# A gated delta rule's chunk inverse with half-column levels, applied once to the values less the state's part

## The chip, the cores and the metric

The kernel runs as one program on one core of a Trainium2 chip. The metric is device time in microseconds (us), the median of several executions.

## The reference

One step of a one-layer hybrid encoder: a combined input projection, latent attention (8 heads), a gated delta rule (4 heads, keys and values of width 128), an output projection and an MLP. It covers a prompt of 16 + 2048 rows and 64 rows of a running stream. The change lies in the delta rule, which the reference evaluates in chunks of `C` rows (the kernel uses 18 chunks: 16 of 128 rows, one of 16, one of 64):

```python
gc = jnp.cumsum(blocks(g), axis=-1)
decay = jnp.exp(jnp.where(causal, gc[..., :, None] - gc[..., None, :], -jnp.inf))
kb = kc * bc[..., None]
a = jnp.where(strict, jnp.einsum('...id,...jd->...ij', kb, kc) * decay, 0.0)
t_inv = lax.linalg.triangular_solve(eye + a, ..., lower=True)      # inverse of I + a
u = t_inv @ (vc * bc[..., None])
w = t_inv @ (kb * jnp.exp(gc)[..., None])
qk = jnp.einsum('...id,...jd->...ij', qc, kc) * decay
def step(S, xs):
    v_new = u_i - w_i @ S
    o = (q_i * jnp.exp(g_i)[..., None]) @ S + qk_i @ v_new
    S = S * jnp.exp(g_last)[..., None] + einsum('bhck,bhcv->bhkv', k_i * jnp.exp(g_last - g_i)[..., None], v_new)
```

## The kernel before

The program runs in stages: input projection (to about 540 us), the delta rule (540 to 966 us), attention over the prompt, attention of the stream, and output projection with MLP. The delta rule is written as generators that a loop in `phase_g` advances by one step a round. `gdn_prep` is independent of the state, and up to four chunks of it are in flight; a new one starts every six rounds. `gdn_scan` carries the state from chunk to chunk, one scan at a time in six steps. The loop also advances the attention's query projection (`q_gen`, 17 tiles, to about 760 us) and then its first keys. The order of a round is only the order in which code is written; a scheduler in the compiler then orders each engine's instructions by its own estimate, and the engines run their queues in that order.

The names: `lev` are the inverse's levels, `tt` and `uu` (`t`, `u` in the code) the inverse so far and its transpose in f16, each for the 4 heads side by side (128 x 512). `m_lv` are 0/1 masks of the levels' blocks. `gpp` (5 buffers) and `gps` (2) are PSUM tiles of the preparation and of the scan. `bn` is minus the masked product of keys with its decay, `bh` and `bl` its f16 high and low part. `dm` are the decays, `lg` the factor from which a product makes their exponents. `kn` are the normalised keys, `kneg` the same times minus the decay, `wt` the inverse applied to `kneg`, `vn` the values, `uf` the finished inverse in f32, `kd` the keys that update the state `S`, `vw` the new values, `o` and `fr` the output and its norm.

A chunk's preparation has six levels (L526 to L541): a product `bh` by `t` (L530), a predicated copy into the next level (L531), two products (L535, L537), and two copies out of PSUM, `t` on ScalarE (L539) and `u` on VectorE (L540). Then a correction makes `uf` (L557), and a product with `kneg` makes `wt` (L561, L563). The scan adds two products in PSUM, `uf` by `vn` (L581) and `wt` by the state (L582), and scales the sum into `vw` (L584).

Of the kernel before, what the change touches and what calls it, by code (L numbers as in the profile page):

```python
# [39 lines left out]
CHUNKS = list(range(NS)) + [17] + list(range(NS, 17))  # L40
# [4 lines left out]
NL = 2  # L45
GL, QLS = 17, 20
GB = {"kq": 4, "qk": 5, "kd": 5, "vn": 5, "uf": 5, "wt": 5, "ss": 5, "kv": 2, "sq": 1, "kn": 1, "lg": 1, "dm": 2, "db": 1, "bn": 1,
      "kneg": 3, "bh": 4, "bl": 4, "tt": 5, "uu": 5, "q16": 2, "rk": 3, "se": 1, "vw": 2, "S": 3, "o1": 1, "o": 1, "fr": 2}
GR, GK, GA, GF = 6, 4, 5, 2
QSB, QS = 2, 5  # L50
# [60 lines left out]
def bc1(ap, p, a, b):  # L111
    return ap.unsqueeze(1).to_broadcast([p, a, b])


def bc2(ap, p, a, b):
    return ap.unsqueeze(2).to_broadcast([p, a, b])


class Prog:
# [318 lines left out]
    def gdn_prep(self, n, P):  # L438

        nc, S = self.nc, self.S  # L440
        t0, C = chunk_span(n)
        sc = self.sc[n]
        want_o = n > 0
        cv = S["convT"].rearrange("(j p) t -> p j t", p=128)
        kv = self.gt("kv", 1, (128, 8, 128))
        nc.sync.dma_start(kv[:, :, :C], cv[:, 4:12, t0:t0 + C])
        kq = self.gt("kq", 2, (128, 4, 2, 128))
        nc.sync.dma_start(kq[:, :, 1, :C], cv[:, 0:4, t0:t0 + C])
        lg = self.gt("lg", 2)
        nc.gpsimd.tensor_tensor(lg[:C, :, :C], bc1(self.m_gt[:C, :C], C, 4, C), bc2(sc["g"][:C], C, 4, C), op=ALU.mult)  # L450
        yield
# [41 lines left out]
        for a in range(2):  # L493
# [31 lines left out]
        while s < C:
            y = lev[i]  # L526
            yield
            ps = self.gpsum()
# [12 lines left out]
            i, s = i + 1, 2 * s  # L541
# [22 lines left out]
        P.update(kq=kq, ss=ss, qk=qk, kd=kd, vn=vn, uf=uf, wt=wt)  # L564

    def gdn_scan(self, n, P):
# [46 lines left out]
        ss = P["ss"]  # L613
# [17 lines left out]
    def phase_g(self, g=True, q=True, eb=None):  # L631

        with ExitStack() as es:
# [1277 lines left out]
```

## Time and profile before

| what | value |
|---|---|
| median of 3 runs | 3350.31 us (3349.01 to 3351.44) |
| the profiled execution's own time, and its span | 3346.45 us, 3344.6 us |
| mean granted TensorE clock | 0.981 of full speed |
| busy, share of the span: PE, DVE, ACT, POOL | 96%, 81%, 47%, 12% |
| the chain that ended last, by engine | PE 84%, DVE 8%, ACT 2%, issue 2%, DMA 2%, POOL 1% |

The span goes from the first to the last instruction; the execution's own time holds 1.85 us more. PE is TensorE (PEld its weight loads), DVE VectorE, ACT ScalarE, POOL GpSimd. A matmul's duration in the trace holds its way through the array, and matmuls overlap; from the start of one to the start of the next is what it costs in a stream. An f32 matmul stands as two instructions.

### The profile page before, as it was taken

How to read it: one execution, taken by the hardware profiler on the slowest of the kernel's cores; microseconds unless marked ns; L12 is line 12 of the kernel's file. 1: busy time of each engine (PE TensorE's matmuls, PEld its weight loads, DVE VectorE, ACT ScalarE, POOL GpSimd, SP SyncE). 2: the span in 40 equal slices, each digit the busy share in tenths (PEclk: the TensorE clock that was granted, in tenths of full speed). 3: DMA queues.
4: the chain of work that ended last, by engine and by line, in shares of the span. 5: the costliest groups of instructions: out<-in, count | busy, mean ns of one | idle time of the engine just before them, and what ended most of it. 6: DMA issues, size and time to landing. Idle time of an engine off the chain costs nothing.

```text
span 3344.6 us, 54489 instructions
## 1 busy us (share of the span) xinstructions
PE 3218.6 (96%) x20037; PEld 2963.2 (89%) x20037; DVE 2693.3 (81%) x5438; ACT 1577.2 (47%) x3495; POOL 400.9 (12%) x758
## 2 busy tenths in 40 slices
PE   9999998998879999999999999999999999999999
PEld 6888887888867878887799999999999999999999
DVE  8877654888868778888689888888988888988887
ACT  5555534565536868787654233334332324422232
POOL 0110014565410000000201000001100002100000
PEclk9999998999989989999999999999999999999999
DMA  4322213233211011110332222234222224122222
GB/s 131 90 73 69 73 66 103 87 96 106 52 56 35 15 34 28 32 40 23 97 98 83 76 74 75 73 88 135 84 72 67 75 76 156 58 76 76 75 74 70
DMA packets 318091, 248.09 MB, mean 74 GB/s; under 512 B 31776, under 2 KB 291616, under 8 KB 317760
## 3 DMA queue, kind: packets, MB, share of 16 engines
q1 hardware_dynamic: 300256, 219.21, 22.5%
q10 hardware_dynamic: 15536, 16.23, 1.6%
q0 software_dynamic: 2032, 9.18, 0.8%
q8 instruction: 157, 2.57, 0.3%
q14 instruction: 110, 0.90, 0.1%
HBM read 196.99 MB, written 47.52 MB: 73 GB/s over the span
## 4 chain that ended last, share of the span: by engine, by line
PE 84%; DVE 8%; ACT 2%; issue 2%; DMA 2%; POOL 1%; ACTq 0%; SPq 0%; POOLq 0%; DVEq 0%
PE psu L1581 23%; PE psd L1581 21%; PE ps L270 5%; PE ps L271 5%; PE ps L272 5%; PE pss L974 2%; PE pso L991 2%; PE pss L975 2%; PE pso L993 2%; PE pss L976 2%; PE pso L992 2%; PE pspre L944 2%; DVE lev L531 1%; DMA qh<-mrow 1%; PE gpp L498 1%
## 5 line engine op out<-in xcount | busy, mean ns | idle before, releaser
L1581 PE MATMUL psu<-hh,uh 128*128 128x352 f32 x1728 | 563.4, 326 | 2.6 <-ACT uh L1477 2.1
L1581 PE MATMUL psu<-hl,uh 128*128 128x352 f32 x1728 | 557.8, 323 | 0.0
L1581 PE MATMUL psu<-hh,ul 128*128 128x352 f32 x1728 | 550.3, 324 | 0.0
L1581 PE MATMUL psd<-al,dh 128*128 128x352 f32 x1536 | 497.1, 324 | 3.3 <-DVE al L1770 3.2
L1581 PE MATMUL psd<-ah,dl 128*128 128x352 f32 x1536 | 495.6, 323 | 0.0
L1581 PE MATMUL psd<-ah,dh 128*128 128x352 f32 x1536 | 473.8, 324 | 11.0 <-DVE y L1689 7.3
L1689 DVE TENSOR_TENSOR y<-y,psd 128x352 f32<-128x352 f32 x768 | 387.6, 516 | 104.1 <-PE psd L1581 102.1
L1581 PEld LDWEIGHTS psu<-hh,uh 128*128 128x128 f32 x1728 | 326.3, 189 | 4.2 <-ACT uh L1477 2.3
L1581 PEld LDWEIGHTS psu<-hl,uh 128*128 128x128 f32 x1728 | 326.5, 189 | 1.2 <-issue 0.5
L1581 PEld LDWEIGHTS psu<-hh,ul 128*128 128x128 f32 x1728 | 324.2, 189 | 0.2 <-DVE ul L1455 0.2
L270 PE MATMUL ps<-hhi,whi 128*128 128x512 f32 (+5 forms) x880 | 313.3, 359 | 10.2 <-ACT hhi L134 7.2
L272 PE MATMUL ps<-hhi,wlo 128*128 128x512 f32 (+5 forms) x880 | 313.9, 357 | 0.0
L271 PE MATMUL ps<-hlo,whi 128*128 128x512 f32 (+5 forms) x880 | 312.4, 356 | 0.3 <-DVE hlo L135 0.2
L1581 PEld LDWEIGHTS psd<-ah,dh 128*128 128x128 f32 x1536 | 284.6, 188 | 16.7 <-DVE y L1689 11.4
L1581 PEld LDWEIGHTS psd<-al,dh 128*128 128x128 f32 x1536 | 289.9, 189 | 5.2 <-DVE al L1770 5.1
L1477 ACT CAST dh<-wr 128x512 fp32r<-128x512 f32 x192 | 119.2, 621 | 368.5 <-PE psd L1581 326.3
L1581 PEld LDWEIGHTS psd<-ah,dl 128*128 128x128 f32 x1536 | 289.6, 189 | 0.0
L1768 ACT CAST ah<-u 128x352 fp32r<-128x352 f32 x192 | 93.4, 487 | 397.6 <-DVE u L1766 279.2
L135 DVE TENSOR_TENSOR Pl<-P,Ph 128x512 fp32r<-128x512 f32 (+4 forms) x352 | 211.7, 611 | 56.8 <-ACT Ph L134 54.3
L978 ACT ACTIVATE P<-pss 128x512 f32<-128x512 f32 (+4 forms) x352 | 185.9, 538 | 94.4 <-PE pss L976 85.6
L945 DVE TENSOR_REDUCE mp<-pspre 128x1 f32<-128x296 f32 (+6 forms) x400 | 189.1, 500 | 35.8 <-PE pspre L944 34.2
L1694 POOL TENSOR_TENSOR y<-y,v 128x352 f32<-128x352 f32 x40 | 40.3, 1030 | 1332.2 <-DVE y L1689 1332.1
(456 smaller groups left out, 7371.1 us busy)
## 6 DMA issues: line engine op xcount, KB each, us to landing
wr<-in_w_up SPq DMA_DIRECT2D x192, 256.0 KB
wr<-in_w_down SPq DMA_DIRECT2D x192, 256.0 KB
qn<-scr_qN SPq DMA_DIRECT2D x32, 384.0 KB
wr<-in_w_out SPq DMA_DIRECT2D x48, 256.0 KB
wraw<-in_w_in SPq DMA_DIRECT2D x42, 256.0 KB
scr_convT<-s SPq DMA_DIRECT2D x36, 256.0 KB
mixr<-scr_mixT SPq DMA_DIRECT2D x12, 704.0 KB
out_y_T<-y SPq DMA_DIRECT2D x48, 176.0 KB
```

The source lines that it names most:

```text
L135: (lo_eng or nc.vector).tensor_tensor(lo, src, hi.bitcast(F32), op=ALU.subtract)
L270: nc.tensor.matmul(ps[:m, :n], whi[:, k, :m], hi[:, k], start=k == 0, stop=False)
L271: nc.tensor.matmul(ps[:m, :n], whi[:, k, :m], lo[:, k], start=False, stop=False)
L272: nc.tensor.matmul(ps[:m, :n], wlo[:, k, :m], hi[:, k], start=False, stop=k == 7)
L944: nc.tensor.matmul(ps[:, :z - a], qh[:r, i * 128:(i + 1) * 128], kh[:r, a:z], start=True, stop=True)
L945: nc.vector.tensor_reduce(m[:, i:i + 1] if one else mp[:, j:j + 1], ps[:, :z - a], axis=AX.X, op=ALU.max)
L974: nc.tensor.matmul(ps[:w, off:], kh[:r, s:s + w], qh[:r, off:], start=True, stop=False)
L978: nc.scalar.activation(p[:w, off:], ps[:w, off:], AF.Exp)
L1477: self.nc.scalar.copy(t[0], src)
L1581: self.nc.tensor.matmul(ps, w, h, start=i == 0, stop=i == len(steps) - 1)
L1689: adds.append(nc.vector.tensor_tensor(Y[j][:, d], Y[j][:, d], ps, op=ALU.add).ins)
L1768: done = nc.scalar.copy(A[f, j][0], u).ins
```

## The change

Four things change in the delta rule.

- At level `i` with block size `s` only every second block of `s` columns is computed: products have 64 moving columns a head in place of 128, and the copies out of PSUM write 64 columns a head in place, into the old `t` and `u`, with strides (`part` picks the blocks). Level 1 still writes a whole new `u`.
- `wt` and `kneg` go. The scan computes keys by state first (`pk`), scales it by minus the decay (`vk`, VectorE), adds the values (`vr`, GpSimd), and applies `uf` to that once.
- The decays' exponents come from one product for the four heads, with the mask as stationary operand and the gate, split into a rounded part `gh` and a rest `gl`, in two moving operands of 512 columns (`fp32r` type). This takes two `lg` tiles a chunk where there was one.
- `kd` is written after the first level, a step boundary in the preparation falls away and one in the scan moves up, and a preparation starts no earlier than four rounds after the last one that uses the same set of level buffers.

```diff
+        nc.scalar.copy(self.sct["gh"], gg)
+        nc.vector.tensor_tensor(self.sct["gl"], gg, self.sct["gh"].bitcast(F32), op=ALU.subtract)
...
-        lg = self.gt("lg", 2)
-        nc.gpsimd.tensor_tensor(lg[:C, :, :C], bc1(self.m_gt[:C, :C], C, 4, C), bc2(sc["g"][:C], C, 4, C), op=ALU.mult)
+        lg = [self.gt("lg", 2, dt=F32R) for _ in range(2)]
+        for x, g in zip(lg, (sc["gh"].bitcast(F32), sc["gl"])):
+            nc.gpsimd.tensor_tensor(x[:C, :, :C], bc1(self.m_le[:C, :C], C, 4, C), bc2(g[:C], C, 4, C), op=ALU.mult)
...
-        for h in range(4):
-            nc.tensor.matmul(pe[:C, h, :C], lg[:C, h, :C], self.m_le[:C, :C], start=True, stop=True)
+        for i, x in enumerate(lg):
+            nc.tensor.matmul(pe[:C, :, :C], self.m_gt[:C, :C], x[:C, :, :C], start=i == 0, stop=i == 1)
...
-        kneg = self.gt("kneg", 1)
-        nc.gpsimd.tensor_tensor(kneg[:C], kn[:C], bc2(sc["negc"][:C], C, 4, 128), op=ALU.mult)
...
+        def part(x, s, e):
+            return x[:C, :, :C].rearrange("p h (b e s) -> p h b e s", e=2, s=s)[:, :, :, e, :]
...
             for h in range(4):
-                nc.tensor.matmul(ps[:C, h, :C], bh[:C, h, :C], t[:C, h, :C], start=True, stop=True)
-            nc.vector.copy_predicated(y[:C, :, :C], bc1(self.m_lv[:C, i + 1, :C], C, 4, C), ps[:C, :, :C])
+                nc.tensor.matmul(ps[:C, h, :H], bh[:C, h, :C], part(t, s, 0)[:, h], start=True, stop=True)
+            nc.vector.copy_predicated(part(y, s, 0), mask(i + 1, s, 0), some(ps))
...
-                nc.tensor.matmul(p1[:C, h, :C], u[:C, h, :C], y[:C, h, :C], start=True, stop=True)
+                nc.tensor.matmul(p1[:C, h, :H], u[:C, h, :C], part(y, s, 0)[:, h], start=True, stop=True)
             for h in range(4):
-                nc.tensor.matmul(p2[:C, h, :C], y[:C, h, :C], u[:C, h, :C], start=True, stop=True)
-            t, u = self.gt("tt", 2, dt=F16), self.gt("uu", 2, dt=F16)
-            nc.scalar.copy(t[:C, :, :C], p1[:C, :, :C])
-            nc.vector.tensor_copy(u[:C, :, :C], p2[:C, :, :C])
+                if i == 1:
+                    nc.tensor.matmul(p2[:C, h, :C], y[:C, h, :C], u[:C, h, :C], start=True, stop=True)
+                else:
+                    nc.tensor.matmul(p2[:C, h, :H], y[:C, h, :C], part(u, s, 1)[:, h], start=True, stop=True)
+            nc.scalar.copy(part(t, s, 0), some(p1))
...
+                nc.vector.tensor_copy(part(u, s, 1), some(p2))
...
-            nc.tensor.matmul(ps[:, h, :C], kneg[:C, h, :], uf[:C, h, :C], start=True, stop=True)
-        wt = self.gt("wt", 2)
-        nc.scalar.copy(wt[:, :, :C], ps[:, :, :C])
...
+        pk = self.gpsum("s")
+        for h in range(4):
+            nc.tensor.matmul(pk[:C, h, :], P["kq"][:, h, 0, :C], st[:, h, :], start=True, stop=True)
+        vk = self.gt("vk", 1)
+        nc.vector.tensor_tensor(vk[:C], pk[:C], bc2(sc["negc"][:C], C, 4, 128), op=ALU.mult)
+        vr = self.gt("vr", 1)
+        nc.gpsimd.tensor_tensor(vr[:C], vk[:C], P["vn"][:C], op=ALU.add)
+        yield
         pv = self.gpsum("s")
         for h in range(4):
-            nc.tensor.matmul(pv[:C, h, :], P["uf"][:C, h, :C], P["vn"][:C, h, :], start=True, stop=False)
-            nc.tensor.matmul(pv[:C, h, :], P["wt"][:, h, :C], st[:, h, :], start=False, stop=True)
+            nc.tensor.matmul(pv[:C, h, :], P["uf"][:C, h, :C], vr[:C, h, :], start=True, stop=True)
...
-                if rounds >= (started - GF) * GR and len(preps) < GK and started < min(len(CHUNKS), scanned + GA):
+                if rounds >= max((started - GF) * GR, began[started % NL] + GL0) and len(preps) < GK and started < min(len(CHUNKS), scanned + GA):
```

The compiled order shows where the work stands now. First VectorE's queue in the middle of the delta rule, around one chunk's new values `vw`, before:

```order
L627 SCALAR_TENSOR_TENSOR o_10339<-gps,g_out,ga 128x512
L531 COPY_PREDICATED lev_4995<-m_lv,gpp 128x512
L531 COPY_PREDICATED lev_4999<-m_lv,gpp 128x512
L485 TENSOR_TENSOR kn<-gpp,rk 128x512
L584 TENSOR_TENSOR vw<-gps,beta 128x512
L540 CAST uu<-gpp 128x512 x2
L590 TENSOR_TENSOR S<-se,gps 128x512
```

And the same place in the change (shapes of three numbers are strided halves, 256 elements a partition):

```order
L648 SCALAR_TENSOR_TENSOR o_9748<-gps,g_out,ga 128x512
L526 COPY_PREDICATED lev_5001<-m_lv,bn 128x512
L598 TENSOR_TENSOR vk<-gps,negc 128x512
L560 CAST uu<-gpp 128x4x64
L560 CAST uu<-gpp 128x32x8
L545 COPY_PREDICATED lev_4998<-m_lv,gpp 128x16x16
L545 COPY_PREDICATED lev_5002<-m_lv,gpp 128x128x2
L474 TENSOR_SCALAR rk<-ss 128x4
L606 TENSOR_TENSOR vw<-gps,beta 128x512
L577 TENSOR_TENSOR uf<-uu,gpp 128x512
L560 CAST uu<-gpp 128x16x16
L612 TENSOR_TENSOR S<-se,gps 128x512
```

The copies of the levels are halves, `vk` is new, and five instructions now stand between `vk` and `vw`. Next GpSimd's queue at the same place of the change, where `vr` is new:

```order
L642 TENSOR_TENSOR o<-o,fr 128x512
L512 TENSOR_TENSOR bl<-bn,bh 128x512
L600 TENSOR_TENSOR vr<-vk,vn 128x512
L455 TENSOR_TENSOR lg<-m_le,gh 128x512
L455 TENSOR_TENSOR lg<-m_le,gl 128x512
L469 AFFINE_SELECT dm<-dm 128x512
```

`vr` stands behind `bl` of a younger chunk; the two `lg` behind it serve the chunk after the one whose `dm` follows. Last, VectorE's queue at the end of the delta rule, before, from the last but one state to the end:

```order
L590 TENSOR_TENSOR S<-se,gps 128x512
L604 TENSOR_TENSOR o_11245<-gps,egc 128x512
L531 COPY_PREDICATED lev_5003<-m_lv,gpp 128x512
L612 TENSOR_TENSOR o<-o_11245,gps 128x512
L540 CAST uu<-gpp 128x512
L618 SCALAR_TENSOR_TENSOR fr<-ss,fr 128x4
L557 TENSOR_TENSOR uf<-uu,gpp 128x512
L627 SCALAR_TENSOR_TENSOR o_11289<-gps,g_out,ga 128x512
L584 TENSOR_TENSOR vw<-gps,beta 128x512
L590 TENSOR_TENSOR S<-se,gps 128x512
```

And in the change from the last but two state on:

```order
L612 TENSOR_TENSOR S<-se,gps 128x512
L625 TENSOR_TENSOR o_10852<-gps,egc 128x512
L577 TENSOR_TENSOR uf<-uu,gpp 128x512
L633 TENSOR_TENSOR o<-o_10852,gps 128x512
L639 SCALAR_TENSOR_TENSOR fr<-ss,fr 128x4
L638 TENSOR_SCALAR fr<-ss 128x4
L648 SCALAR_TENSOR_TENSOR o_10919<-gps,g_out,ga 128x512
L598 TENSOR_TENSOR vk<-gps,negc 128x512
L606 TENSOR_TENSOR vw<-gps,beta 128x512
L612 TENSOR_TENSOR S<-se,gps 128x512
```

The last inverse (`uf`) is done one scan earlier than before, so that the last two scans have no preparation beside them.

## Rows read from the trace of the kernel before

**Rows 1.** Busy time by stretch: us, then busy and instructions per engine, clock, DMA.

```profile
550.00:600.00 50.00, 44.57 (x305) 38.00 (x306) 34.10 (x68) 25.74 (x79) 34.40 (x56) 0.74 0.27 76
...
836.20:856.40 20.20, 17.02 (x188) 15.92 (x186) 17.15 (x29) 10.35 (x36) 10.04 (x18) 1.00 0.27 67
```

**Rows 2.** VectorE's queue in order of time: the state's updates, first, fifteenth, last ones.

```profile
614.67 0.67 DVE L590 TENSOR_TENSOR S<-se,gps 128x512 f32<-128x512 f32 x1
...
916.33 0.69 DVE L590 TENSOR_TENSOR S<-se,gps 128x512 f32<-128x512 f32 x1
...
945.97 0.69 DVE L590 TENSOR_TENSOR S<-se,gps 128x512 f32<-128x512 f32 x1 [0.65 <-PE gps L588]
...
958.20 0.69 DVE L590 TENSOR_TENSOR S<-se,gps 128x512 f32<-128x512 f32 x1 [1.32 <-PE gps L588]
...
966.37 0.75 DVE L627 SCALAR_TENSOR_TENSOR o<-gps,g_out,ga 128x512 f32<-128x512 f32 x1 [3.98 <-PE gps L625]
```

**Rows 3.** Groups by shape, VectorE and TensorE, 530 to 980 us: busy, mean ns, idle before.

```profile
L540 DVE CAST uu<-gpp 128x512 f16<-128x512 f32 x96 | 63.4, 681 | 10.6 <-PE gpp L537 10.4
...
L531 DVE CAST_PREDICATED lev<-m_lv,gpp 128x512 f16<-128x512 uint8 x96 | 63.0, 681 | 10.1 <-PE gpp L530 10.1
...
L531 DVE CAST_PREDICATED lev<-m_lv,gpp 64x256 f16<-64x256 uint8 x5 | 2.0, 405 | 0.0
...
L530 PE MATMUL gpp<-tt,bh 64*64 64x64 f16 x20 | 1.5, 198 | 0.0
```

**Rows 4.** VectorE's queue in one period: start, us, instruction, idle before.

```profile
839.65 0.41 DVE L502 TENSOR_TENSOR qk<-gpp,dm 128x256 f32<-128x256 f32 x1
839.98 1.28 DVE L531 CAST_PREDICATED lev<-m_lv,gpp 128x512 f16<-128x512 uint8 x2
841.17 0.41 DVE L500 TENSOR_TENSOR bn<-gpp,db 128x256 f32<-128x256 f32 x1
...
855.47 0.69 DVE L584 TENSOR_TENSOR vw<-gps,beta 128x512 f32<-128x512 f32 x1 [0.56 <-PE gps L582]
```

**Rows 5.** GpSimd's queue in the same period.

```profile
842.32 1.15 POOL L511 TENSOR_TENSOR bl<-bn,bh 128x512 f16<-128x512 f32 x1 [2.96 <-ACT bh L510]
...
847.40 1.04 POOL L450 TENSOR_TENSOR lg<-m_gt,g 128x512 f32<-128x512 f32 x1
```

**Rows 6.** TensorE's queue in order of time: products by kind.

```profile
300.15 0.39 PE L270 MATMUL ps<-hhi,whi 128*128 128x512 f32 x1
300.38 0.39 PE L271 MATMUL ps<-hlo,whi 128*128 128x512 f32 x1
...
598.83 0.31 PE L521 MATMUL gpp<-id,lev 64*64 64x64 f16 x4 [0.24 <-DVE lev L517]
...
841.37 0.39 PE L535 MATMUL gpp<-lev,uu 128*128 128x128 f16 x4
841.59 0.39 PE L537 MATMUL gpp<-uu,lev 128*128 128x128 f16 x4
...
846.10 1.06 PE L461 MATMUL gpp<-m_le,lg 128*128 128x128 f32 x8
846.99 0.39 PE L555 MATMUL gpp<-uu,q 128*128 128x128 f16 x4
...
850.20 0.95 PE L482 MATMUL gpp<-ones,sq 128*128 128x1 f32 x8
851.02 0.63 PE L625 MATMUL gps<-ident,o 128*128 128x128 f32 x4
```

**Rows 7.** TensorE's queue at the end of the delta rule.

```profile
958.95 1.16 PE L610 MATMUL gps<-vw,qk 128*128 128x128 f32 x8
965.22 1.11 PE L625 MATMUL gps<-ident,o 128*128 128x128 f32 x4 [5.11 <-POOL o L621]
```

**Rows 8.** Stretches of 5 us there; columns as in rows 1.

```profile
955.00:960.00 5.00, 4.22 (x35) 3.79 (x33) 2.23 (x4) 0.00 (x0) 0.80 (x1) 1.00 0.40 105
...
965.00:970.00 5.00, 3.62 (x11) 2.54 (x11) 3.63 (x12) 1.61 (x4) 1.12 (x5) 0.50 0.21 69
```

More of the change, by code (lines that the diff above doesn't have):

```diff
@@ L46 @@
 GL, QLS = 17, 20
-GB = {"kq": 4, "qk": 5, "kd": 5, "vn": 5, "uf": 5, "wt": 5, "ss": 5, "kv": 2, "sq": 1, "kn": 1, "lg": 1, "dm": 2, "db": 1, "bn": 1,
-      "kneg": 3, "bh": 4, "bl": 4, "tt": 5, "uu": 5, "q16": 2, "rk": 3, "se": 1, "vw": 2, "S": 3, "o1": 1, "o": 1, "fr": 2}
-GR, GK, GA, GF = 6, 4, 5, 2
+GB = {"kq": 4, "qk": 5, "kd": 5, "vn": 5, "uf": 5, "ss": 5, "kv": 2, "sq": 1, "kn": 1, "lg": 2, "dm": 2, "db": 1, "bn": 1,
+      "vk": 2, "vr": 2, "bh": 4, "bl": 4, "tt": 5, "uu": 5, "q16": 2, "rk": 3, "se": 1, "vw": 2, "S": 3, "o1": 1, "o": 1, "fr": 2}
+GR, GK, GA, GF, GL0 = 6, 4, 5, 2, 4
 QSB, QS = 2, 5
@@ L378, in gdn_consts @@
         t = lambda name, shape, dt=F32: c.tile(list(shape), dt, name=name)
-        self.m_le, self.m_gt = t("m_le", (128, 128)), t("m_gt", (128, 128))
+        self.m_le, self.m_gt = t("m_le", (128, 128)), t("m_gt", (128, 128), F32R)
         self.m_lv = t("m_lv", (128, 8, 128), U8)
@@ L385, in gdn_consts @@
         self.nc.gpsimd.memset(self.bt, 0.0)
-        self.sct = {k: t(k, (128, nch, 4)) for k in ("beta", "nbeta", "g", "egc", "negc", "egl")}
+        self.sct = {k: t(k, (128, nch, 4)) for k in ("beta", "nbeta", "g", "egc", "negc", "egl", "gl")}
+        self.sct["gh"] = t("gh", (128, nch, 4), F32R)
         self.sc = {n: {k: v[:, i, :] for k, v in self.sct.items()} for i, n in enumerate(CHUNKS)}
@@ L502, in gdn_prep @@
                 nc.vector.tensor_tensor(qk[:C, 2 * a:2 * a + 2, :C], ghv[:C, :, 1, :C], dm[:C, 2 * a:2 * a + 2, :C], op=ALU.mult)
-        kneg = self.gt("kneg", 1)
-        nc.gpsimd.tensor_tensor(kneg[:C], kn[:C], bc2(sc["negc"][:C], C, 4, 128), op=ALU.mult)
-        kd = self.gt("kd", 2)
-        nc.gpsimd.tensor_tensor(kd[:C], kn[:C], dm[:C, :, C - 1:C].to_broadcast([C, 4, 128]), op=ALU.mult)
         bh = self.gt("bh", 1, dt=F16)
@@ L515, in gdn_prep, with mask @@
                 nc.vector.tensor_copy(y, bc1(self.id16, 128, 4, 128))
+        def part(x, s, e):
+            return x[:C, :, :C].rearrange("p h (b e s) -> p h b e s", e=2, s=s)[:, :, :, e, :]
+        def mask(i, s, e):
+            m = self.m_lv[:C, i, :C].rearrange("p (b e s) -> p b e s", e=2, s=s)[:, :, e, :]
+            return m.unsqueeze(1).to_broadcast([C, 4, C // (2 * s), s])
         u = lev[0]
         nc.vector.copy_predicated(u[:C, :, :C], bc1(self.m_lv[:C, 1, :C], C, 4, C), bn[:C, :, :C])
+        kd = self.gt("kd", 2)
+        nc.gpsimd.tensor_tensor(kd[:C], kn[:C], dm[:C, :, C - 1:C].to_broadcast([C, 4, 128]), op=ALU.mult)
         yield
@@ L527, in gdn_prep @@
             yield
+            H = C // 2
+            some = lambda ps: ps[:C, :, :H].rearrange("p h (b s) -> p h b s", s=s)
             ps = self.gpsum()
             for h in range(4):
-                nc.tensor.matmul(ps[:C, h, :C], bh[:C, h, :C], t[:C, h, :C], start=True, stop=True)
-            nc.vector.copy_predicated(y[:C, :, :C], bc1(self.m_lv[:C, i + 1, :C], C, 4, C), ps[:C, :, :C])
+                nc.tensor.matmul(ps[:C, h, :H], bh[:C, h, :C], part(t, s, 0)[:, h], start=True, stop=True)
+            nc.vector.copy_predicated(part(y, s, 0), mask(i + 1, s, 0), some(ps))
             yield
@@ L534, in gdn_prep @@
             for h in range(4):
-                nc.tensor.matmul(p1[:C, h, :C], u[:C, h, :C], y[:C, h, :C], start=True, stop=True)
+                nc.tensor.matmul(p1[:C, h, :H], u[:C, h, :C], part(y, s, 0)[:, h], start=True, stop=True)
             for h in range(4):
-                nc.tensor.matmul(p2[:C, h, :C], y[:C, h, :C], u[:C, h, :C], start=True, stop=True)
-            t, u = self.gt("tt", 2, dt=F16), self.gt("uu", 2, dt=F16)
-            nc.scalar.copy(t[:C, :, :C], p1[:C, :, :C])
-            nc.vector.tensor_copy(u[:C, :, :C], p2[:C, :, :C])
+                if i == 1:
[3 more added lines that the diff above has]
+            nc.scalar.copy(part(t, s, 0), some(p1))
+            if i == 1:
+                u = self.gt("uu", 2, dt=F16)
+                nc.vector.tensor_copy(u[:C, :, :C], p2[:C, :, :C])
+            else:
+                nc.vector.tensor_copy(part(u, s, 1), some(p2))
             i, s = i + 1, 2 * s
@@ L557, in gdn_prep @@
         nc.vector.tensor_tensor(uf[:C, :, :C], u[:C, :, :C], ps[:C, :, :C], op=ALU.add)
-        yield
-        ps = self.gpsum()
-        for h in range(4):
-            nc.tensor.matmul(ps[:, h, :C], kneg[:C, h, :], uf[:C, h, :C], start=True, stop=True)
-        wt = self.gt("wt", 2)
-        nc.scalar.copy(wt[:, :, :C], ps[:, :, :C])
-        P.update(kq=kq, ss=ss, qk=qk, kd=kd, vn=vn, uf=uf, wt=wt)
+        P.update(kq=kq, ss=ss, qk=qk, kd=kd, vn=vn, uf=uf)
     def gdn_scan(self, n, P):
@@ L598, in gdn_scan @@
             return
-        yield
         po = self.gpsum("s")
@@ L646, in phase_g @@
             preps, scan, started, scanned, rounds = [], None, 0, 0, 0
+            began = [-GL0] * NL
             while g and scanned < len(CHUNKS):
-                if rounds >= (started - GF) * GR and len(preps) < GK and started < min(len(CHUNKS), scanned + GA):
+                if rounds >= max((started - GF) * GR, began[started % NL] + GL0) and len(preps) < GK and started < min(len(CHUNKS), scanned + GA):
                     preps.append(self.gdn_prep(CHUNKS[started], Ps[started]))
+                    began[started % NL] = rounds
                     started += 1
```

## The prediction

> **What bounds the kernel now.** First the page's chain of waits: TensorE holds 84% of it, because most of the program (projection, attention, MLP) is a dense stream of products. The change touches none of that, so the table of busy time by stretch comes next. In the delta rule [rows 1] TensorE and VectorE are both busy for about 17 of 20.2 us (17.02 and 17.15), while ScalarE and GpSimd are busy for half of it. The stretch is one period of the stage, the time from one chunk to the next. It shows two queues run in order, each almost full, whose gaps of 3 us are waits for each other. VectorE's queue gives the pace of the whole stage: the state is updated first at 614.67 us and for the fifteenth time at 916.33 [rows 2], so 14 periods take 301.7 us, 21.5 us each. They are longer than 20.2 in the first half, where the query projection and the first keys run beside them. Before 614 us lies a start of 70 us, in which VectorE is busy for two thirds of the time and the granted clock averages 0.74 [rows 1]; it waits for short chains rather than for one engine. At the very end the scan stands almost alone: 12.2 us from the last but one state to the last, and 8.2 us to the last output [rows 2].
>
> So what the change is worth is what one period gets shorter, times 14, with a start and an end that follow other rules.
>
> **VectorE, per chunk of 128.** By shape, a copy out of PSUM of 512 elements takes 681 ns, and the 64-row chunk shows the predicated copy with 256 elements at 405 ns [rows 3]. In the queue they overlap a little: two copies started at 839.98 take until 841.17, so 0.60 us each, and 256 elements step by 0.33 (839.65 to 839.98) [rows 4]. A half therefore saves 0.26 us. The change halves six predicated copies and five of the six copies of `u`: 11 x 0.26 = 2.9 us. It adds `vk`, which has the form of `vw` (PSUM by a broadcast scalar, 0.69 us [rows 4]) and costs a step of 0.6. Net: 2.3 us less. The trace has no copy with pieces of two to sixteen elements. The bound on one side is the contiguous half (0.26 saved), on the other the full copy (nothing saved); I take the first, since the 256-element rows are the same engine, type and element count and differ only in the pattern.
>
> **TensorE, per chunk.** `wt` goes: eight instructions. `pk` and the new single product take 16 instructions where `uf` by `vn` and `wt` by state took 16, so they cancel. A group of eight f32 instructions costs 0.89 us from its start to the next one's (846.10 to 846.99) [rows 6]. The exponents' eight (0.89) become two of 512 columns at 0.23 each (300.15 to 300.38) [rows 6], 0.43 less. Then 68 f16 products (24 at L530, 24 at L535, 20 at L537) have 64 moving columns in place of 128. Now they step by 0.055 us (four in 0.22, 841.37 to 841.59) [rows 6]. Nearest rows on either side: with 64 x 64 weights and 64 columns, four products last 0.31 [rows 6] where a single one takes 198 ns [rows 3], so some 0.037 a step; and the f32 product with a single moving column still steps by 0.10 (eight in 0.82, 850.20 to 851.02), hardly less than with 128 columns, which says that a full weight load can set the step by itself [rows 6]. So each saves between 0 and 0.018 us; I take 0.010, near the middle, 0.7 us in all. Sum: 0.89 + 0.43 + 0.7 = 2.0 us, between 1.3 and 2.5.
>
> The Trainium skill (TensorE: Matmul & The Clock Gate, LDWEIGHTS) has a weight load take time by the stationary operand's columns and not by what moves, about 107 ns for 128. The trace disagrees with the figure (one load and one product together step by 55 ns), but not with the rule behind it; by that rule the 68 products would save nothing and TensorE's sum would be 1.3 us.
>
> **The other two engines.** ScalarE loses `wt`'s copy and half of six others; it is idle half the time [rows 1], so this buys nothing by itself. GpSimd loses `kneg` and gains `vr` and a second `lg`, about 1.04 us each [rows 5]: 1.05 us more on 10.0 of 20.2. The `lg` are written a period ahead of their product, which hides them; without that cover, 1.04 us a chunk.
>
> **The new chain in the scan.** `vk`, `vr` and the product with `uf` now stand between state and `vw`. `vr` cannot start before `bl` of a younger chunk is through (1.15 us [rows 5]), and behind `vw` wait `uf`, a copy and the state. Between `vk` and `vw` VectorE has four halves and `rk`, 1.4 to 2 us of work. From `vk`'s end, `vr` takes 1.04, and eight products until the result some 1.16 [rows 7], with two handovers about 2.3. VectorE already waits 0.56 at `vw` [rows 4]; so this wait stays about what it is. I cost it at nothing more.
>
> **The period.** VectorE 17.15 - 2.3 = 14.9, TensorE 17.0 - 2.0 = 15.0; both fall alike, and the mutual gaps of 3 us have no reason to change. I take 2.2 us a period, 14 x 2.2 = 31 us.
>
> **Start and end.** A first preparation is some 22 steps in 70 us, 3 us each; one step less, and a chunk's cheaper products on top, shorten the start by 0 to 5 us, and since a later start of the third preparation works against it I take 2. The end gets longer. The last `uf` is done a scan earlier, so two scans stand alone. One such loop: state to transposition 7.0 us (958.20 [rows 2] to 965.22 [rows 7]), transposition 0.6, `pk`, `pv` and the state's product 1.16 each, `vk` and `vw` 0.69 each, `vr` 1.04, six handovers of about 0.08: 14.0 where 12.2 stand, so 3.5 for two. And where TensorE sat idle for 5.1 us the granted clock went from 1.00 to 0.50 [rows 7, 8], that is to 1.2 GHz. In the change such a gap comes in each of the lone scans. At half clock four products of the transposition took 1.11 in place of 0.63 [rows 6, 7]; for eight that is 0.9 more, and four and a half such groups lie on the loop: 4 us a scan, for none to two scans. I take the end at +6, between +2 and +12.
>
> **Sum.** -31 - 2 + 6 = -27 us: 3319 us against the profiled execution's 3346.45, which lies 4 us below the median of the three runs; 3350 - 27 = **3323 us**. The stages behind start earlier as a whole, but the scheduler has also put attention's instructions in another order in places; I know no sign for that and allow 5 us either way.
>
> **Rivals.**
> (a) *Weight loads set the step.* TensorE falls only to 15.7 and becomes the one bound; 1.3 x 14 = 18, so -18 - 2 + 6 = -14, 3336. For it: the one-column row. Against it: 64 x 64 at 0.037.
> (b) *The gaps shrink too*, since each engine's wait is for the other's halved work: 3.0 a period, -42 - 4 + 5 = -41, 3309. For it: VectorE sat idle for 10.6 and 10.1 us before the two copies of the levels, for products that get shorter [rows 3], over 16 chunks 1.3 us each, of which 0.8 would go. Against it: `vk` and `vr` add waits of their own.
> (c) *The scan's new chain is the bound.* If `vr` sits behind `bl` and TensorE's queue delays `pv`, `vw` waits 1.5 to 2 us longer and all but 0.3 us of a period's gain is given back: -4 - 2 + 6 = 0, 3350. It decides once `vw` waits over 2 us.
> (d) *Pieces of few elements run at the full copy's price or worse.* Then VectorE has 0.6 more a period: 8 - 2 + 6 = +12, 3362, slower. It decides from a step of 0.52 us for a half on, where 11 halves save 0.9, just what `vk` and the longer end (4 us over 14 periods) cost. The Trainium skill (SBUF — State Buffer, Door 1: The DMA port swizzle, on cachelines) says that an access crossing to a new 16-byte line pays, and that two hits a line suffice; the smallest pieces leave four f16 values a line, so by it this would not happen. No run here shows it yet.
> (e) *The halves are not halves*: the compiled order shows 256 elements, so this is out.
>
> **Numbers.** Forecast (3312 to 3331) 0.50, (a) 0.20, (b) 0.12, (c) 0.10, (d) 0.08. The range takes in (a) and (b) with the 5 us of reordering: 3304 to 3342. A measurement of this kernel can tell about 0.2%, 6.7 us, from no change. Forecast, (a) and (b) give faster: 0.82; (c) gives the same: 0.10; (d) slower: 0.08.
>
> **What the profile after would show.** Halves near 0.41 us in both forms, whatever the pieces (0.6 or more: (d)). f16 products of 64 columns stepping by 0.045 (0.055: (a)). Fourteen periods in about 270 us (301.7 now). VectorE's wait at `vw` below 1 us (over 2: (c)). The last two states about 14 us apart at full clock, 18 at half. If periods shorten as forecast and the total does not, the loss is in the end or in attention's new order.

## The result, and the profile after

The changed kernel takes 3380.59 us (median of 4, 3377.73 to 3385.55) where the kernel before took 3349.66 beside it (4 runs): 1.0094, 95% interval 1.0076 to 1.0111. It is slower by 31 us; the forecast was 27 us faster. A few executions, of several kernels, took far longer (5833 us and more) and are left out of every ratio; the profiled execution of kq5_no_decays is one of them, so that run has no row in the table below.

VectorE's queue, the state's updates (answers to [rows 2]):

```profile
601.72 0.69 DVE L612 TENSOR_TENSOR S<-se,gps 128x512 f32<-128x512 f32 x1 [0.27 <-PE gps L610]
...
930.21 0.68 DVE L612 TENSOR_TENSOR S<-se,gps 128x512 f32<-128x512 f32 x1
...
960.97 0.69 DVE L612 TENSOR_TENSOR S<-se,gps 128x512 f32<-128x512 f32 x1 [2.17 <-PE gps L610]
...
978.48 0.69 DVE L612 TENSOR_TENSOR S<-se,gps 128x512 f32<-128x512 f32 x1 [2.24 <-PE gps L610]
...
986.95 0.75 DVE L648 SCALAR_TENSOR_TENSOR o<-gps,g_out,ga 128x512 f32<-128x512 f32 x1 [3.98 <-PE gps L646]
```

The start is 13.0 us shorter (614.67 to 601.72), the 14 periods take 328.5 us in place of 301.7, the end 56.7 in place of 50.0. The stage ends 20.6 us later; the span is 34.9 longer (3379.5), so 14.3 more are lost behind the stage.

Of the 26.8 us by which the periods got longer, 26 lie in the first eight. These stretches before and after, with the columns of [rows 1]:

```profile
614.67:798.23 183.56, 173.36 (x1648) 158.14 (x1648) 160.17 (x311) 107.75 (x355) 117.01 (x235) 1.00 0.37 104
601.72:811.37 209.65, 173.65 (x1645) 156.57 (x1645) 167.39 (x344) 103.37 (x376) 134.82 (x256) 0.93 0.33 96
```

TensorE is busy as long as before, though its products got shorter, and its clock is 0.93 in place of 1.00. VectorE has 344 instructions in place of 311; 8 are `vk`, most others work of the preparations and the query projection that the earlier first state leaves behind it. The ninth state comes 13 us later (811.4, 798.2).

The instructions themselves became as short as forecast. Groups by shape, 530 to 980 us ([rows 3]), and TensorE's queue ([rows 6]):

```profile
L545 DVE CAST_PREDICATED lev<-m_lv,gpp 128x256 f16<-128x256 uint8 x96 | 38.2, 421 | 9.4 <-PE gpp L544 9.3
...
L560 DVE CAST uu<-gpp 128x256 f16<-128x256 f32 x80 | 32.0, 413 | 6.6 <-PE gpp L554 6.4
...
L487 PE MATMUL gpp<-ones,sq 128*128 128x1 f32 x128 | 19.2, 271 | 13.5 <-ACT sq L484 13.5
```

```profile
877.45 2.07 PE L503 MATMUL gpp<-kq 128*128 128x256 f32 x4
...
882.32 0.28 PE L549 MATMUL gpp<-lev,uu 128*128 128x64 f16 x4
882.44 0.28 PE L554 MATMUL gpp<-uu,lev 128*128 128x64 f16 x4
```

Halves take 421 and 413 ns whatever their pieces; the f16 products of 64 columns step by 0.030 us (four in 0.12), where 0.045 was taken. New is the wait of L487, the sums of squares of the queries. Stretches ([rows 1]), the start's, one period's, and two of 5 us:

```profile
550.00:600.00 50.00, 41.11 (x356) 34.10 (x357) 34.72 (x77) 26.08 (x85) 34.93 (x64) 0.91 0.33 91
870.20:889.40 19.20, 15.57 (x173) 14.11 (x172) 13.30 (x29) 8.93 (x33) 11.23 (x19) 0.91 0.29 71
870.00:875.00 5.00, 2.67 (x27) 2.47 (x26) 3.27 (x5) 1.27 (x3) 4.05 (x8) 1.00 0.55 143
875.00:880.00 5.00, 5.00 (x49) 4.31 (x50) 2.38 (x9) 2.66 (x13) 1.96 (x6) 0.69 0.07 19
```

VectorE has 13.3 us of work in a period of 19.2, and TensorE's clock, 1.00 in [rows 1], is 0.91. The chain of waits through that period (start, us, what):

```profile
869.05 1.16 PE gps L610 x8
870.21 0.91 PE gps L623 x8
871.19 3.10 DMA kq<-scr_convT
874.31 0.64 ACT sq L484
875.00 1.05 PE gpp L487 x8
...
876.31 0.47 PE gpp L494 x4
...
877.64 1.88 PE gpp L503 x4
...
882.61 1.45 DVE lev L526
...
887.50 0.70 DVE vw L606
888.24 1.16 PE gps L610 x8
```

`kq` has four buffers. The scan's last reader of one is L623; only then is it loaded for the chunk four places on (3.1 us), and that chunk's Square (L484) and products (L487) stand close behind L623 in the queues of ScalarE and TensorE. So every queue waits. TensorE sat idle for 2.33 us before L487; in the 5 us behind this gap its clock is 0.69, a mixture of 1.2 and 2.4 GHz, and four products of L503 take up to 2.07 us (1.03 and 1.08 before, at 838.24 and 839.55). Before, the same load was issued right behind its reader too, but ended long before its use:

```profile
837.35 1.06 PE L602 MATMUL gps<-S,kq 128*128 128x128 f32 x8
...
838.44 0.36 SPq L448 DMA_DIRECT2D kq<-scr_convT  x1
...
847.79 0.65 ACT L479 ACTIVATE sq<-kq 128x512 f32<-128x512 f32 x1
```

So the Square started 10.4 us behind the reader then, and starts 4.3 us behind it now. The idle time that ended with this load in all (600 to 980 us), and that of `vw`:

```profile
ACT sq L484 <- DMA kq<-scr_convT: 10.8, 9, 1.9
...
DVE vw L606 <- PE gps L604: 8.0, 5, 3.5
```

That is ScalarE's idle time alone. On the chain of waits the load itself holds 20.8 us, 17.4 of them between the ninth and the fifteenth state, 2.8 to 3.1 in each of these six periods.

### The profile page after: what moved, and what is told of

The parts are those of the page before. It is cut to its first block, busy times and chain, and to the rows that moved or that the text cites. A ratio compares the mean times of both kernels' runs of the same rounds, so it can differ in the third digit from the quotient of the medians.

```text
span 3379.5 us, 54048 instructions
## 1 busy us (share of the span) xinstructions
PE 3204.8 (95%) x19785; PEld 2944.0 (87%) x19785; DVE 2664.7 (79%) x5457; ACT 1551.9 (46%) x3478; POOL 422.2 (12%) x776
## 4 chain that ended last, share of the span: by engine, by line
PE 82%; DVE 9%; DMA 3%; ACT 3%; issue 2%; POOL 2%; SPq 0%; POOLq 0%; ACTq 0%; DVEq 0%
PE psu L1605 23%; PE psd L1605 20%; PE ps L270 5%; PE ps L271 5%; PE ps L272 5%; PE pss L998 2%; PE pso L1015 2%; PE pss L999 2%; PE pss L1000 2%; PE pso L1017 2%; PE pso L1016 2%; PE pspre L968 2%; DMA kq<-scr_convT 1%; DMA qh<-mrow 1%; PE gps L610 1%
```

## The experiments

All were compared with the kernel before on the same chip. Columns: the first S in us; S 1 to 9, S 9 to 15, S 15 to the last output, and from there to the span's end, in the profiled execution.

| run | median us | ratio, 95% | S 1 at | 1-9 | 9-15 | end | behind |
|---|---|---|---|---|---|---|---|
| before | 3349.66 | | 614.7 | 183.5 | 118.1 | 50.0 | 2378.2 |
| changed | 3380.59 | 1.0094 (1.0076, 1.0111) | 601.7 | 209.7 | 118.8 | 56.7 | 2392.5 |
| kq5 | 3361.02 | 1.0026 (1.0015, 1.0037) | 601.4 | 208.7 | 101.9 | 59.4 | 2381.6 |
| levels_alone | 3347.46 | 0.999 (0.998, 1.0) | 608.3 | 180.3 | 121.4 | 48.5 | 2385.5 |
| scan_alone | 3387.98 | 1.0112 (1.0095, 1.0129) | 604.8 | 213.8 | 126.2 | 59.0 | 2381.5 |
| no_decays | 3366.67 | 1.0045 (1.0027, 1.0062) | 599.3 | 201.4 | 120.8 | 56.7 | 2388.6 |
| scan_kq5 | 3362.94 | 1.0032 (1.0018, 1.0046) | 604.8 | 200.7 | 127.0 | 58.8 | 2373.0 |
| kq5_vr_vector | 3352.23 | 1.0005 (0.999, 1.0019) | 603.2 | 204.0 | 112.1 | 53.7 | 2375.0 |
| kq5_vr_vector_no_decays | 3322.49 | 0.9921 (0.9906, 0.9936) | 599.3 | 190.7 | 106.5 | 48.9 | 2377.8 |
| levels_buffers | 3312.09 | 0.9898 (0.9881, 0.9916) | 605.3 | 181.4 | 105.3 | 46.9 | 2369.5 |
| buffers_alone | 3342.38 | 0.9981 (0.9968, 0.9995) | 606.4 | 183.7 | 122.1 | 48.7 | 2381.9 |
| scan_kq5_vr_vector | 3347.94 | 0.9993 (0.9975, 1.0012) | 599.4 | 212.0 | 111.7 | 49.8 | 2372.8 |
| levels_buffers_decays | 3336.03 | 0.996 (0.9945, 0.9975) | 608.7 | 190.4 | 110.9 | 49.6 | 2373.3 |
| decays_high_only | 3330.79 | 0.994 (0.9917, 0.9963) | 597.5 | 192.5 | 102.6 | 49.2 | 2380.1 |
| no_start_rule | 3360.44 | 1.0036 (1.0022, 1.0051) | 598.9 | 208.3 | 119.0 | 56.7 | 2371.1 |
| levels_buffers_lg_scalar | 3330.43 | 0.9936 (0.9913, 0.9959) | 604.8 | 181.1 | 113.4 | 49.8 | 2379.3 |
| levels_o1 | 3345.09 | 0.9981 (0.9968, 0.9993) | 607.4 | 184.2 | 121.9 | 47.2 | 2383.7 |
| vr_vector_no_decays_o1 | 3326.78 | 0.993 (0.9909, 0.9951) | 598.5 | 189.8 | 103.5 | 49.9 | 2379.7 |
| mended_change | 3372.53 | 1.0057 (1.0037, 1.0078) | 597.4 | 222.3 | 123.2 | 48.9 | 2378.5 |

The scheduler makes a new order for nearly every edit, and an order alone is worth up to 20 us (no_start_rule, below). So a single pair proves little under 20 us; several pairs with one sign, or a wait that can be read, prove more. Two runs with the same order (levels_alone, levels_o1) differ by up to 4 us in a column.

**The wait for `kq`, and the parts by themselves.**

```diff
-GB = {"kq": 4, ... "vk": 2,
+GB = {"kq": 5, ... "vk": 1,
```

Expected of kq5:

> The changed kernel with five kq buffers in place of four (one vk buffer instead of two makes the room). In the changed kernel the reload of kq waits for the scan's product L623, and the Square L484, the product L487 and what is queued behind them wait for that load; the granted clock falls to 0.50 in the gaps. Theory kq: without that wait the period falls from 19.8 us to about 17.7 as forecast, the clock stays at 1.00 in 800:900, the stage ends 25 to 30 us earlier, and the time is 3335 to 3355. Rival clock: the halved products alone leave TensorE too little to do, the gaps stay and move, 3370 to 3382. Rival scan chain (state to pk to vk to vr to pv): the period stays at 19.8, 3375 to 3385.

Measured 3361, 20 us better; no wait for `kq` is left. S 9 to 15 take 17 us less, as much as the load held of the chain there, and three periods in a row are 15.9 us with the clock back at 1.00 (this is one of them):

```profile
862.30:878.20 15.90, 14.17 (x172) 12.85 (x172) 12.30 (x29) 8.52 (x33) 11.34 (x19) 1.00 0.31 80
```

For these periods the rival that short products alone let the clock fall is out. But S 1 to 9 are no better, with the clock at 0.93 there as in the changed kernel, nor is the end, and the time is 6 us above the expected range.

The parts: the level loop's hunks alone on the kernel before (levels_alone); the scan's hunks alone (scan_alone); and the changed kernel with the decays' lines as before, the split of the gate among them (no_decays):

```diff
-        lg = [self.gt("lg", 2, dt=F32R) for _ in range(2)]
-        for x, g in zip(lg, (sc["gh"].bitcast(F32), sc["gl"])):
-            nc.gpsimd.tensor_tensor(x[:C, :, :C], bc1(self.m_le[:C, :C], C, 4, C), bc2(g[:C], C, 4, C), op=ALU.mult)
+        lg = self.gt("lg", 2)
+        nc.gpsimd.tensor_tensor(lg[:C, :, :C], bc1(self.m_gt[:C, :C], C, 4, C), bc2(sc["g"][:C], C, 4, C), op=ALU.mult)
...
-        for i, x in enumerate(lg):
-            nc.tensor.matmul(pe[:C, :, :C], self.m_gt[:C, :C], x[:C, :, :C], start=i == 0, stop=i == 1)
+        for h in range(4):
+            nc.tensor.matmul(pe[:C, h, :C], lg[:C, h, :C], self.m_le[:C, :C], start=True, stop=True)
```

Expected of levels_alone:

> The kernel before with the half-column levels alone; scan, wt and decays as before. Theory kq (the loss comes from where the scan's products now stand against the reload of kq): the order around kq is that of before, so VectorE's 2.9 us a period come through in part or whole, 3312 to 3340. Rival clock (half-column products make TensorE's idle longer and its clock fall): 3350 to 3385.

Expected of scan_alone:

> The kernel before with the inverse applied once, to the values less the state's part (pk, vk, vr in place of kneg and wt; one turn less in the scan), levels and decays as before. Theory kq: this part holds the loss, 3360 to 3390, with a wait of 2 us or more for kq's load in most periods. Rival clock: the products and their number are nearly those of before, so nothing is lost: 3335 to 3355. Rival scan chain: 3355 to 3385, with vw or pv waiting over 2 us a chunk and none of it for kq.

Expected of no_decays:

> The changed kernel with the decays' sums as before (four products of 128 columns in FP32 per chunk, one lg tile). Theory kq: the wait stays, 3375 to 3392. Rival: the two lg products on GpSimd and their split are late and hold the order, then 3340 to 3365 without them.

The scan's part holds a loss by itself (3388): ScalarE waits 13.8 us for `kq` there, in no_decays 19.8, in levels_alone 1.2. Levels alone are 3 us faster, at the edge of the noise, which neither theory had. And without the decays' product 14 us come back, although the wait stays, which the first theory had not either: a second cause.

```diff
-GB = {"kq": 4,
+GB = {"kq": 5,
```

Expected of scan_kq5 (that edit on scan_alone):

> Scan alone with five kq buffers (kneg and wt, now gone, left the room). Theory kq: the waits for kq's load, 2.8 to 3.1 us on the chain in each late period, go, as they did in the changed kernel: 3355 to 3372 instead of 3388. Rival: they give way to the next wait (vr on GpSimd, the sums of squares): 3378 to 3390.

3363, 25 us less and in the theory's range, again with no wait for `kq`. But the gain is not where the wait was. In scan_alone the load holds 17.9 us of the chain in S 9 to 15, and this stretch does not get shorter (126.2, then 127.0); `vr` on GpSimd, 1.3 us of the chain there before, holds 6.3, as the rival had it. The time comes from S 1 to 9 and from behind the stage, which a new order moves too. So this pair does not show the price of the wait a second time.

**GpSimd's queue: `vr` and the second `lg`.**

```diff
-        vk = self.gt("vk", 1)
-        nc.vector.tensor_tensor(vk[:C], pk[:C], bc2(sc["negc"][:C], C, 4, 128), op=ALU.mult)
...
-        nc.gpsimd.tensor_tensor(vr[:C], vk[:C], P["vn"][:C], op=ALU.add)
+        for h in range(4):
+            nc.vector.scalar_tensor_tensor(vr[:C, h], pk[:C, h], sc["negc"][:C, h:h + 1], P["vn"][:C, h], ALU.mult, ALU.add)
```

Expected of kq5_vr_vector:

> The changed kernel with five kq buffers, and vk and vr as one step on VectorE (four of 128x128, straight from PSUM) in place of VectorE's vk and GpSimd's vr. Theory GpSimd: what is still lost with five kq buffers lies in the first eight intervals of S (209 us there, 184 before) and comes from GpSimd's queue, which has 1.28 us more of vr and 1.05 us more of lg in each chunk; without vr they take 190 to 202, the lone scans at the end 1 to 1.5 us less each, and the time is 3335 to 3352. Rival order: the first half is lost to the order of the query stage's work, not to GpSimd; 206 to 212, time 3354 to 3364.

Expected of scan_kq5_vr_vector (the same edit on scan_kq5):

> scan_kq5 (3363) with vk and vr as one step on VectorE. Theory GpSimd: vr's 1.28 us on GpSimd and its hop are what the scan change still costs, 3338 to 3355. Rival: VectorE's 0.2 us more a chunk and the order take it back, 3356 to 3368.

Times 9 and 15 us lower, at the edge of and inside their ranges, but not where the theory put them: S 1 to 9 take 204.0 (190 to 202 expected) and even 212.0 after 200.7. The gain is in the lone scans (59.4 to 53.7, 58.8 to 49.8) and, in scan_kq5_vr_vector, in S 9 to 15: with the load gone, `vr` was the next wait there (127.0 to 111.7).

Expected of kq5_no_decays (kq5 with the decays' lines as before):

> The changed kernel with five kq buffers and the decays' sums as before (one lg on GpSimd, four FP32 products). Theory GpSimd: the first eight intervals of S take 195 to 203 instead of 209; the later ones stay at 16 to 18; time 3340 to 3355. Rival order: 206 to 212 in the first eight, and 0.4 us more of TensorE in each chunk: 3358 to 3370.

It took 3356.30 (1.0018; 1.0006 to 1.003), between the two ranges and 5 us less than kq5, with intervals that overlap.

Expected of kq5_vr_vector_no_decays (both edits):

> Both: five kq buffers, vr on VectorE and the decays' sums as before, so that GpSimd has 2.1 us less in each chunk than in the changed kernel and the same as before less kneg. Theory GpSimd: the first eight intervals take 180 to 190, as before the change or less, and the time is 3320 to 3342. Rival order: 200 or more, time 3350 to 3365.

3322, 30 us less than kq5_vr_vector, the time in its range, S 1 to 9 at 190.7 just above.

```diff
-        lg = [self.gt("lg", 2, dt=F32R) for _ in range(2)]
-        for x, g in zip(lg, (sc["gh"].bitcast(F32), sc["gl"])):
+        lg = [self.gt("lg", 2, dt=F32R) for _ in range(1)]
+        for x, g in zip(lg, (sc["gh"].bitcast(F32), )):
```

Expected of decays_high_only:

> kq5_vr_vector (3352) with the low part of the split decays left out: one lg on GpSimd and one product instead of two (one lg buffer). Theory GpSimd: as with the decays of before, 3315 to 3330. Rival: it is the order, not GpSimd's second lg: 3342 to 3356.

3331, at the edge of its range: 21 us less than kq5_vr_vector. This run leaves out the gate's low part and keeps the new form of the product, and the one before it has the old form; what they share is a single `lg`. A place where it may hurt shows in the queues of kq5_vr_vector, GpSimd's, and ScalarE's exponential between:

```profile
662.55 1.04 POOL L455 TENSOR_TENSOR lg<-m_le,gh 128x512 fp32r<-128x512 f32 x1 [3.62 <-PE gpp L466]
663.54 1.04 POOL L455 TENSOR_TENSOR lg<-m_le,gl 128x512 fp32r<-128x512 f32 x1
...
664.13 0.62 ACT L468 ACTIVATE dm<-gpp 128x512 f32<-128x512 f32 x1
...
664.54 1.02 POOL L135 TENSOR_TENSOR ql_l<-ql_r,ql_h 128x384 fp32r<-128x384 f32 x1
...
665.91 0.63 POOL L469 TENSOR_SCALAR_AFFINE_SELECT dm<-dm 128x512 f32<-128x512 f32 x1
```

Both `lg` are for the next chunk, a period ahead of their product. But they stand in front of this chunk's `dm`, here with two pieces of the query projection between (`ql_l` is one), and later in the stage with nothing between. The exponential of `dm` is done at 664.75, and `dm` starts 1.16 later. Over the chunks between 600 and 900 us that delay is 0.95 us on average here, 0.93 in the changed kernel and 1.00 in scan_kq5 (which has `vr` and one `lg`), against 0.20 in kq5_vr_vector_no_decays, 0.15 in decays_high_only and 0.24 in scan_kq5_vr_vector. That this delay is the cost is not shown: the kernel before has 0.64, kq5's three periods of 15.9 us have 1.1 to 1.3, and scan_kq5_vr_vector has the longer S 1 to 9 (212.0 against 200.7) with the shorter delay.

**The levels' own worth.**

```diff
-GB = {"kq": 4, ... "wt": 5, ... "o1": 1,
+GB = {"kq": 5, ... "wt": 2, ... "o1": 2,
```

Expected of levels_buffers (on levels_alone):

> The kernel before with the half-column levels, and with buffers moved: wt 2 instead of 5, kq 5 instead of 4, o1 2 instead of 1 (its one tile waits for mixT's store, 3.85 us twice between 820 and 930 in levels alone). Theory buffers: the periods of S between 788 and 910, 17.0 to 24.4 in levels alone, become 16 to 18 throughout, the stage ends 10 to 15 us earlier, 3328 to 3340. Rival clock (with half-column products TensorE's gaps and the fall of its clock take the gain): 3344 to 3356.

Expected of buffers_alone (on the kernel before):

> The kernel before with the buffers of levels_buffers (wt 2, kq 5, o1 2) and nothing of the change. Theory: the half-column levels earn the 38 us once the order and the waits let them; then the buffers alone give little here, 3338 to 3352, with VectorE and TensorE both near 17 us a period as before. Rival: the buffers (or the order that the compiler makes with them) earn it alone: 3308 to 3328.

Expected of levels_o1 (`o1` 2 and `wt` 4 on levels_alone):

> Levels alone with two o1 buffers (wt 4 makes the room); the order of the instructions on every engine is that of levels alone, so this shows the o1 wait by itself. Theory o1: the two waits of 3.85 us for mixT's store between 820 and 930, and what falls in behind them, go: 3330 to 3342. Rival: they are made up for behind the stage, 3343 to 3349, and the gain of levels_buffers comes from the order that it has.

Expected of vr_vector_no_decays_o1:

> Five kq buffers, vr on VectorE and the decays' sums as before, now with two o1 buffers (uf 3 makes the room); the order of the instructions on every engine is that of kq5_vr_vector_no_decays. Theory o1: the wait of o1 for mixT's store is part of what is left, 3308 to 3318. Rival: it is hidden, 3319 to 3325.

3312 against 3342: with that room the levels earn 28 to 30 us (by the ratios, by the medians), and levels_buffers, 16 us below its range, beats both kernels, by 1.0% the one before. The two runs with `o1` alone have unchanged orders and moved by 2 us down and 4 us up: the wait for `mixT`'s store (3.85 us twice on the chain of levels_alone, none in levels_o1) is made up for. So the rest comes with the fifth `kq` buffer or with `wt` at two, though levels_alone hardly waits for `kq`. By elimination it is the order that the scheduler makes with them; what in that order does it stays open.

The decays' hunks on levels_buffers (`o1` back to 1), the changed kernel without its rule on starts (first edit), and `lg` on ScalarE (second edit, for levels_buffers; in mended_change both parts, on kq5_vr_vector):

```diff
-GR, GK, GA, GF, GL0 = 6, 4, 5, 2, 4
+GR, GK, GA, GF, GL0 = 6, 4, 5, 2, 0
...
-            nc.gpsimd.tensor_tensor(x[:C, :, :C], bc1(self.m_le[:C, :C], C, 4, C), bc2(g[:C], C, 4, C), op=ALU.mult)
+            for h in range(4):
+                nc.scalar.activation(x[:C, h, :C], self.m_le[:C, :C], AF.Copy, scale=g[:C, h:h + 1])
```

Expected of levels_buffers_decays:

> levels_buffers (3312) with the decays' sums as one product per chunk in two parts (o1 back to one buffer for the room, which earlier changed nothing). Theory GpSimd: 1.05 us more on GpSimd in each chunk lies on the way from lg to pe and dm, while TensorE saves 0.43: 3318 to 3342, slower than without. Theory of the forecast: TensorE's saving counts, 3300 to 3312.

+24 us. The decays' product costs time in four pairs clear of the noise (14, 21, 24, 30 us), with 8 to 13 us of it in S 1 to 9 each time; in the fifth (5 us, kq5) it is not clear.

Expected of no_start_rule:

> The changed kernel with GL0 at 0, so that the third chunk may start in round 0 and not 4; the same instructions in another order. Theory kq: the wait for kq's load stays, 3370 to 3390. Rival: the rule delayed the first chunks and with them all, 3350 to 3368.

20 us less with the same instructions, in the rival's range but not by its mechanism, since the first state comes only 2.8 us earlier. In the profiled executions 4 us are won in the stage, where the wait for `kq` stays (15.1 us of ScalarE's time, and 31.4 of the chain where the changed kernel has 20.8, so that wait and time do not go one for one), and 21 behind it. By the count of attention's score products the changed kernel falls 17 us behind between 1290 and 1420 us; TensorE's stretches there, in the changed kernel:

```profile
1320.00:1330.00 10.00, 7.47 (x34) 5.88 (x33) 5.89 (x19) 5.55 (x17) 0.13 (x1) 0.70 0.15 41
1380.00:1390.00 10.00, 8.94 (x37) 6.93 (x36) 7.29 (x19) 5.91 (x13) 0.00 (x0) 0.78 0.15 44
1390.00:1400.00 10.00, 10.00 (x34) 7.70 (x33) 7.82 (x14) 6.16 (x11) 0.00 (x0) 0.71 0.00 0
```

The clock is 0.70 to 0.78, each time with a load of `mrow` of 1.6 to 2.3 us on the chain of waits just before or in the stretch; without the rule all stretches from 1280 to 1460 have 1.00. Both kernels wait for `mrow` about equally (7.7 and 7.4 us in all), so the amount does not explain it; why the clock falls at these two and not at others stays open.

Expected of levels_buffers_lg_scalar:

> levels_buffers (3312) with lg made on ScalarE, four of 128x128 a chunk, in place of one on GpSimd; decays' products as before. Theory GpSimd: 1.05 us less on GpSimd a chunk, 3296 to 3310. Rival: without vr and the second lg GpSimd is no longer late, or ScalarE's 1 us more takes it back: 3308 to 3322.

Expected of mended_change:

> The whole change with five kq buffers, vr in one step on VectorE, and both lg parts on ScalarE (eight of 128x128 a chunk) in place of GpSimd. Theory GpSimd: 2.1 us less there a chunk against kq5_vr_vector (3352), so as good as decays_high_only (3331) or better: 3312 to 3332. Rival: ScalarE, which also serves the levels, is now late: 3340 to 3356.

Both miss both of their ranges, 18 and 20 us slower than without (13 and 17 by the ratios), so the test from the other side failed. GpSimd's delay of `dm` is gone (0.21 and 0.16 us), but a part of `lg` takes ScalarE four times 0.42, 1.67 us and not 1. The chain of mended_change shows where they went:

```profile
862.33 0.49 PE gpp L461 x4
862.84 0.48 ACT sq L464 x3
...
864.33 0.93 ACT lg L456 x3
865.50 1.28 ACT lg L456 x4
867.04 0.54 ACT sq L485
867.62 1.43 PE gpp L488 x8
```

They stand in front of the same Square and sums that the load of `kq` had held.

## Why the prediction was wrong

Between the forecast (-27) and the profiled executions (+34.9) lie 62 us: 44 in S 1 to 9, 14 in S 9 to 15, 14 behind the stage and 1 at the end, less 11 that the start gained.

- **The step that failed** is "the mutual gaps of 3 us have no reason to change". From S 9 to 15 the work fell as forecast, TensorE's to 15.6 us a period (14.2 at full clock in kq5), VectorE's to 13.3, but a load of `kq` of some 3 us entered each period and the clock fell behind it: 118.8 us, the 118.1 of before. Without it they took 101.9, that is 2.7 us a period less than before, between the 2.2 of the forecast and the 3.0 of rival (b). The prediction priced each moved instruction, but neither the load that waits for a buffer's last reader nor what the new order puts next behind that load. The Trainium skill (Perfetto Trace Analysis, Optimization Strategy) reads a gap that repeats as a possible lack of room for the next tile; in these periods the trace agrees, and one tile of 4 kB a partition was worth 17 us of them.
- **The first eight periods** are the largest part of the miss: 26 us longer, where the same step forecast some 18 less. The fifth buffer gave 1 us there in the changed kernel. In the scan's part alone it gave 13, but scan_alone's waits for `kq` on the chain begin only at 797 us, so most of it is not this wait. Levels alone take 180.3, so the loss comes with the scan's part (200.7 with five buffers, 17 us) and with the second `lg` (8 to 13).
- **"The `lg` are written a period ahead of their product, which hides them"** is in doubt too: hidden from the product, not from `dm` behind them in GpSimd's queue. The order printed ahead of the prediction shows it, `lg`, `lg`, `dm`. The prediction's price for a lost cover, 1.04 us a chunk, stands beside the 0.4 to 0.8 by which `dm` is later than in the same kernel with one `lg`; a single `lg` delayed it before as well (0.64).
- **Halves and steps** were right or too cautious: 421 and 413 ns, 0.030 a step. In kq5's period VectorE has 12.30 and TensorE 14.17 us of work, where 14.9 and 15.0 were forecast; of the 17.15 that the forecast began with, 0.9 was a wait for GpSimd (last section). Rivals (a) and (d) are out.
- **The scan's chain** was right as far as `vw` goes: beside preparations it waited 0.9 us at most, and over 2 us, rival (c)'s mark, only in the two lone scans (2.59 and 3.51).
- **The end** was +6.7 (forecast +6), and as reasoned: the last two states are 17.5 us apart at a mean clock of 0.60, between the 14 and 18 given. **The start** was -13 and not -2, mis-sized: outside the 0 to 5 given, with the clock at 0.91 in place of 0.74. Much of that needs nothing of the change: buffers_alone starts 8 us earlier too.
- **Behind the stage** 5 us either way was too little: 14.3, and 21 between two orders of the same work.

Shown is that the late periods of the changed kernel waited for `kq` and lost 17 us by it, and that the second `lg` costs time; the size of the latter, 14 to 30 us where it is clear, goes with the order. That it costs by the delay of `dm` is argued and not shown. What the scan's part does to S 1 to 9 stays open: it is not the wait for `kq`, and `vr` on VectorE did not cure it alone.

## What to carry to other kernels

Before pricing the instructions of a change, list each buffer whose last reader or next user moves, when it is loaded again, and what stands next in the queues that wait for it; a full pool can turn a saved step into a wait for a load. When a wait is taken out, see whether the time is won where the wait was, or elsewhere. An instruction that is early for its own reader may still be late for its neighbour in an in-order queue. Where a scheduler rebuilds the order, test parts in several surroundings and size the order's luck with an edit that leaves the work alone.

## What the runs showed of the hardware

VectorE's copy of level 0, with all operands in SBUF, takes 0.68 us in some periods and 1.53 to 1.67 in others. In the longer ones GpSimd's `bl` had started just before it (0.04 to 0.2 us in eight of nine). The changed kernel, then kq5, then the period of [rows 4] before, whose `bl` [rows 5] shows at 842.32:

```profile
863.15 1.16 POOL L512 TENSOR_TENSOR bl<-bn,bh 128x512 f16<-128x512 f32 x1 [3.15 <-ACT bh L511]
863.33 1.53 DVE L526 CAST_PREDICATED lev<-m_lv,bn 128x512 f16<-128x512 uint8 x1
```

```profile
870.77 0.69 DVE L526 CAST_PREDICATED lev<-m_lv,bn 128x512 f16<-128x512 uint8 x1
871.18 1.29 POOL L512 TENSOR_TENSOR bl<-bn,bh 128x512 f16<-128x512 f32 x1 [1.04 <-ACT bh L511]
```

```profile
842.43 1.58 DVE L517 CAST_PREDICATED lev<-m_lv,bn 128x512 f16<-128x512 uint8 x1
```

In these rows the one that starts second takes longer, so 0.9 us hang on the order of the two. One copy does not fit (at 753.49, 0.68 us, with `bl` recorded from 0.43 before it; there `bl` took 2.13). The Trainium skill (SBUF — State Buffer, Who interferes with whom) has the two engines share a port pair as an exclusive lock, held for a whole instruction; the rows shown agree.
